# An 8192 x 8192 float32 transpose: two whole-row loads by GpSimd replaced by 26 small ones

## The chip, the core and the metric

The kernel runs on one core of one Trainium2 chip. The time is that of the device for one execution, in microseconds (us). The core has five engines that work side by side: TensorE (PE in the profile; its weight loads are PEld), VectorE (DVE), ScalarE (ACT), GpSimd (POOL) and SyncE (SP), which here only issues transfers. Transfers between the chip's memory and the core's on-chip memory run on 16 DMA engines. An instruction on SyncE puts a transfer into one queue (q1 in the profile, "SPq" where it is issued), one on GpSimd into another (q0, "POOLq"); both queues are served by the same 16 DMA engines. A transfer raises a semaphore by 16 in all when it has landed, one count for each DMA engine.

## The reference

```python
def setup_inputs():
    return {
        "x": np.random.randn(8192, 8192).astype(np.float32),
    }

def reference(x: np.ndarray) -> np.ndarray:
    return np.transpose(x)
```

256 MB (268.44 MB in the profile's unit) are read and as many written.

## The kernel before

**Tiling.** `x` is cut into T = 128 chunks of 128 rows by J = 4096 columns, 2048 KB each: chunk t holds the rows of c = t mod 64 and the left (t < 64) or right half of the columns. A chunk is loaded into a place of `arena`, 128 partitions of 16 KB. It has 16 ranges of 256 columns. TensorE transposes each range in two blocks of 128 x 128 against the identity `ident` (line 414), always every second column, into one of two PSUM tensors: ranges 0 to 7 into `pss[0]`, 8 to 15 into `pss[1]`. ScalarE empties the first and VectorE the second (`copies`, line 341), either into `slots`, where blocks wait, or straight into the place of the store that is next. VectorE then gathers what has been waiting into that place (`gather`, line 303). A store w (`store`, issued through `wide_dma`, line 28) writes one range of the last 16 chunks, 2048 KB again, so each of the 16 ranges is written every 16 chunks. At the start and the end, and where the left half turns into the right, stores are smaller or in two parts.

**Order.** SyncE issues everything in one order, made ahead: store t - 1, then load t + 2 (more loads ahead in the first ten chunks), and so on. It waits before each: before a store until its pieces have been copied, before a load until the place in `arena` is free (`free`, line 206). Such a wait holds up everything behind it on SyncE. `home` says where in `arena` a load or store lies, `before` whose place it takes over.

**Semaphores.** `s_ld` has one semaphore for each place of a chunk; a landed load adds 16, and TensorE waits for 16 and takes them away. `s_pe` counts TensorE's progress, 4 a chunk (5 in the last). `s_free` hands PSUM back to TensorE. In the chunks from E = 12 to LAST TensorE also runs two filler matmuls a chunk (line 408) on a PSUM tensor not in use, and from chunk 24 on ScalarE makes two filler copies a chunk (line 450) once the chunk has landed.

**The two loads apart.** Chunks 40 and 88 (`APART`) are loaded another way (`load_apart`). GpSimd loads PART = 120 of the 128 rows itself (line 231), SyncE the other 8 (line 234); GpSimd waits for both and then adds 16 to `s_ld` in the transfers' stead (line 240). Ahead of chunk 40, at the start of the kernel (line 394), GpSimd makes a load of 5 rows of 64 numbers into `spare`, and right ahead of chunk 88 one of 1 row (line 219, in `turn_engines`), and waits for its landing. Nothing reads `spare`. Apart from `ident`, made in the first microseconds, GpSimd has no other work.

## Time and profile before

| | us |
|---|---|
| median of 3 runs | 1283.3 |
| lowest and highest of them | 1281.83 and 1286.52 |
| the profiled execution | 1285.68 |
| its span, from the first to the last instruction | 1283.9 |
| mean granted clock of TensorE in it | 0.877 |

The page of the profile gives first each engine's busy time, its share of the span and its count of instructions. Then the span is cut into 40 equal slices of 32.1 us. In the rows of the engines and of DMA a digit is the busy share of a slice in tenths; GB/s is what the 16 DMA engines moved in it. The rows of the queues give packets, MB and the time that the packets took, as a share of the time of 16 engines. A group of instructions is shown as line, engine, operation, what it writes and reads, how often, then busy us, the mean ns of one, and how long the engine was idle before them. In a timeline a row is start, length, engine, line and operation; a "q" behind the engine means that its sequencer issued a transfer. In a view by stretches a row is the stretch, its length, each engine's busy time (and count of instructions), then the granted clock, the busy share of the 16 DMA engines and GB/s. It puts a packet wholly into the stretch in which it starts, so a share can be a little over 1.

### The profile page before, as it was taken

The page shows a single profiled execution, that of the slowest core. Times are in us where ns is not written, and L with a number is a line of the kernel's source. Part 1 is how long each engine was busy: PE and PEld are TensorE (multiplying, and loading weights), DVE is VectorE, ACT ScalarE, POOL GpSimd, SP SyncE. Part 2 cuts the span into 40 slices and gives each one's busy share as a digit, 9 for nine tenths or more (in the row PEclk, how much of TensorE's full clock was granted, in tenths as well). Part 3 has the DMA queues.
Part 4 walks back from the last instruction along what each step waited for, and adds up shares of the span by engine and source line. Part 5 has one row for each costly group of instructions (what it writes and reads, how often), then busy time and mean ns, then how long its engine had stood idle before and what let it go on. Part 6 is the DMA issues. An engine that isn't in the chain of part 4 may idle for free. (4 is left out here: it accounts for less than half of the span.)

```text
span 1283.9 us, 12050 instructions
## 1 busy us (share of the span) xinstructions
PE 850.2 (66%) x4552; PEld 648.6 (51%) x4552; DVE 614.8 (48%) x715; ACT 638.7 (50%) x606; POOL 4.0 (0%) x10
## 2 busy tenths in 40 slices
PE   6767777666656776677666776676666676666630
PEld 6655555544445555455445554455555554545430
DVE  3554544554444454454445544444544545445471
ACT  2321215566455556655655556555665555655510
POOL 0000000000000000000000000000000000000000
PEclk9988888989889888988899889879889978899865
DMA  9999999999999999999999999999999999999998
GB/s 395 414 427 431 429 431 430 431 428 431 359 403 417 431 431 431 430 432 430 428 429 429 424 422 430 382 402 430 432 432 429 430 423 403 426 429 419 407 384 336
DMA packets 41430, 537.10 MB, mean 418 GB/s; under 512 B 4672, under 2 KB 5312, under 8 KB 8384
## 3 DMA queue, kind: packets, MB, share of 16 engines
q1 hardware_dynamic: 41056, 532.96, 98.5%
q0 software_dynamic: 352, 3.93, 1.1%
q14 instruction: 18, 0.15, 0.0%
q8 instruction: 4, 0.07, 0.0%
HBM read 268.44 MB, written 268.44 MB: 418 GB/s over the span
## 5 line engine op out<-in xcount | busy, mean ns | idle before, releaser
L414 PEld LDWEIGHTS ps<-ident,arena 128*128 128x128 f32 x4096 | 559.0, 211 | 251.3 <-issue 250.6
L414 PE MATMUL ps<-ident,arena 128*128 128x128 f32 x4096 | 574.3, 304 | 138.9 <-PEq L411 138.9
L303 DVE COPY arena<-slots 128x2048 f32<-128x2048 f32 (+7 forms) x316 | 304.1, 1011 | 519.3 <-DMA out_dram<-arena 511.5
L408 PE MATMUL ps<-ident 128*128 128x512 f32 x456 | 282.4, 752 | 247.3 <-PEq L406 247.3
L450 ACT COPY ps<-ident 128x2048 f32<-128x2048 f32 x204 | 381.4, 1869 | 68.4 <-DMA arena<-in_x_dram 64.7
L341 ACT COPY slots<-ps 128x1024 f32<-128x1024 f32 (+2 forms) x335 | 238.3, 781 | 244.6 <-DVE arena L303 226.9
L341 DVE COPY slots<-ps 128x512 f32<-128x512 f32 (+2 forms) x336 | 289.2, 911 | 57.8 <-PE ps L414 56.4
L408 PEld LDWEIGHTS ps<-ident 128*128 128x128 f32 x456 | 89.5, 217 | 336.3 <-issue 336.3
L341 ACT COPY arena<-ps 128x256 f32<-128x256 f32 x66 | 24.5, 372 | 282.8 <-DVE arena L303 238.4
L341 DVE COPY arena<-ps 128x256 f32<-128x256 f32 x63 | 26.7, 424 | 69.5 <-PE ps L414 68.7
L231 POOL DMA_DIRECT2D arena<-in_x_dram x2 | 2.1, 1056 | 338.2 <-PE ps L414 332.6
L219 POOL DMA_DIRECT2D spare<-in_x_dram x2 | 1.1, 574 | 481.3 <-PE ps L414 481.1
L341 ACT ACT_TABLE_LOAD x1 | 1.3, 1283 | 1.0 <-SPq L160 1.0
L385 POOL TENSOR_SCALAR_AFFINE_SELECT ident<-ident 128x128 f32<-128x128 f32 x1 | 0.3, 287 | 0.2 <-POOL ident L383 0.2
L383 POOL MEMSET ident<- 128x128 f32 x1 | 0.2, 204 | 0.5 <-SPq L160 0.5
L492 POOL MEMSET const-bfloat16-1.0<- 128x1 bf16 x1 | 0.1, 101 | 0.0
L492 POOL MEMSET const-uint8-127<- 128x1 uint8 x1 | 0.1, 101 | 0.0
L492 POOL MEMSET const-float32-0.0<- 128x1 f32 x1 | 0.1, 98 | 0.2 <-issue 0.2
L492 POOL MEMSET const-float32-1.0<- 128x1 f32 x1 | 0.1, 98 | 0.0
## 6 DMA issues: line engine op xcount, KB each, us to landing
arena<-in_x_dram SPq DMA_DIRECT2D x126, 2048.0 KB, 20.3
out_dram<-arena SPq DMA_DIRECT2D x98, 2048.0 KB, 16.7
out_dram<-arena SPq DMA_DIRECT2D x4, 1920.0 KB, 12.3
out_dram<-arena SPq DMA_DIRECT2D x4, 1792.0 KB, 12.3
out_dram<-arena SPq DMA_DIRECT2D x4, 1664.0 KB, 13.2
out_dram<-arena SPq DMA_DIRECT2D x4, 1536.0 KB, 13.8
out_dram<-arena SPq DMA_DIRECT2D x4, 1408.0 KB, 13.1
out_dram<-arena SPq DMA_DIRECT2D x4, 1280.0 KB, 15.3
```

Of the source, the lines that this page charges most:

```text
L219: nc.gpsimd.dma_start(out=spare[:n, :], in_=x[:n, :64]).then_inc(s_gp, 16)
L231: nc.gpsimd.dma_start(out=arena[:PART, o:o + J], in_=x[c * P:c * P + PART, s * J:(s + 1) * J]).then_inc(s_gp, 16)
L303: cp = nc.vector.tensor_copy(out=ap(arena, do, [[P, len(v)], [dist, B], [1, P]]), in_=ap(slots, so, [[gap, len(v)], [P, B], [1, P]]),)
L341: cp = eng.copy(out=dst, in_=i) if e == 0 else eng.tensor_copy(out=dst, in_=i)
L383: nc.gpsimd.memset(ident, 0.0).then_inc(s_id, 1)
L385: nc.gpsimd.affine_select(out=ident, in_=ident, compare_op=mybir.AluOpType.not_equal, fill=1.0, base=0, pattern=[[-1, P]], channel_multipl ...
L408: nc.tensor.matmul(out=pss[1][:, :4 * P], lhsT=ident, rhs=four, start=True, stop=True)
L414: tr = nc.tensor.transpose(pss[h][:, (u * B + b) * P:(u * B + b + 1) * P], arena[:, q + b:q + PIECE - B + b + 1:B], ident,)
L450: cp = nc.scalar.copy(out=pss[0].rearrange("p (k i) -> p k i", i=P), in_=ap(ident, 0, [[0, J // 2 // P], [1, P]]))
L492: nc = _bacc.Bacc("TRN2", target_bir_lowering=False, num_devices=1)
```

## The change

Chunks 40 and 88 are loaded as all others are. `load_apart`, `turn_engines` and the semaphore `s_few` go. In place of the load of 5 rows at the start stands `small_loads`: GpSimd waits until TensorE is through with chunk 39 + k (k = 0 to 25; `s_pe` at 4 x (40 + k)), loads the first n rows and m columns of `x` into `spare`, and waits for the landing. `spare` becomes twice as wide. The 26 loads have between 1 and 120 rows, of 17 to 128 numbers.

```diff
-        spare = nc.alloc_sbuf_tensor("spare", [P, 64], dt).ap()
+        spare = nc.alloc_sbuf_tensor("spare", [P, 128], dt).ap()
...
-        s_few = nc.alloc_semaphore("s_few")
...
-        APART = (40, 88)
-        PART = P - P // 16
-        gp = [0]
-
-        def turn_engines(n):
-            nc.gpsimd.dma_start(out=spare[:n, :], in_=x[:n, :64]).then_inc(s_gp, 16)
-            gp[0] += 16
-            nc.gpsimd.wait_ge(s_gp, gp[0])
-
-        def load_apart(t):
-            s, c = divmod(t, CH)
-            o = home["L", t] * PIECE
-            for u in before["L", t]:
-                free(nc.sync, u)
-                free(nc.gpsimd, u)
-            if t > APART[0]:
-                turn_engines(1)
-            nc.gpsimd.dma_start(
-                out=arena[:PART, o:o + J], in_=x[c * P:c * P + PART, s * J:(s + 1) * J]
-            ).then_inc(s_gp, 16)
-            nc.sync.dma_start(
-                out=arena[PART:, o:o + J], in_=x[c * P + PART:(c + 1) * P, s * J:(s + 1) * J]
-            ).then_inc(s_few, 16)
-            gp[0] += 16
-            nc.gpsimd.wait_ge(s_gp, gp[0])
-            nc.gpsimd.wait_ge(s_few, 16 * (APART.index(t) + 1))
-            nc.gpsimd.sem_inc(s_ld[home["L", t]], 16)
+        FIRST = 40
+        shapes = [(n, 64) for n in (15, 30, 60, 90, 120, 105, 75, 45, 12, 24, 36, 48, 72, 7, 14, 28, 56, 112, 100)]
+        shapes += [(1, 17), (1, 34), (15, 64), (13, 64), (4, 64), (15, 128), (30, 128)]
+
+        def small_loads():
+            for k, (n, m) in enumerate(shapes):
+                nc.gpsimd.wait_ge(s_pe, 4 * (FIRST + k))
+                nc.gpsimd.dma_start(out=spare[:n, :m], in_=x[:n, :m]).then_inc(s_gp, 16)
+                nc.gpsimd.wait_ge(s_gp, 16 * (k + 1))
...
-            if t in APART:
-                load_apart(t)
-                return
...
-        turn_engines(5)
+        small_loads()
```

## The prediction

> **What bounds the kernel now.** I read the page first: the share of each engine, the slices, the DMA queues, the chain that ended last.

> ```profile
> span 1283.9 us, 12050 instructions
> PE 850.2 (66%) x4552; PEld 648.6 (51%) x4552; DVE 614.8 (48%) x715; ACT 638.7 (50%) x606; POOL 4.0 (0%) x10
> ...
> DMA  9999999999999999999999999999999999999998
> GB/s 395 414 427 431 429 431 430 431 428 431 359 403 417 431 431 431 430 432 430 428 429 429 424 422 430 382 402 430 432 432 429 430 423 403 426 429 419 407 384 336
> ...
> q1 hardware_dynamic: 41056, 532.96, 98.5%
> q0 software_dynamic: 352, 3.93, 1.1%
> ```

> No compute engine is busy for more than 66% of the span, while the packets of the SP queue (q1) alone fill 98.5% of the time of the 16 DMA engines. The kernel moves 537 MB, and in its undisturbed slices it moves them at 430 to 432 GB/s. So time is lost only where the GB/s row falls below 431, and it falls at the start, at slices 11 to 13 (from 321 us), at slices 26 and 27 (from 802 us) and at the end. The two holes in the middle are where chunks 40 and 88 are loaded. The busy row stays at 9 in them: the engines were not idle there, their packets took longer.

> Next I cut the span into stages at these holes. The columns behind the colon are the length, busy time and count of each engine, then the granted clock, the DMA share and GB/s.

> ```profile
> core 0: us, PE busy (x) PEld busy (x) DVE busy (x) ACT busy (x) POOL busy (x), PEclk, DMA share, GB/s
> 140.00:336.00 196.00, 134.32 (x720) 101.56 (x720) 96.71 (x112) 92.86 (x93) 0.54 (x1) 0.90 1.01 430
> 336.00:404.40 68.40, 42.69 (x216) 32.05 (x216) 27.95 (x32) 34.48 (x31) 0.00 (x0) 0.83 1.00 377
> 404.40:614.00 209.60, 150.09 (x760) 108.14 (x760) 102.11 (x117) 124.11 (x108) 0.00 (x0) 0.88 1.01 431
> 614.00:818.00 204.00, 140.08 (x752) 105.75 (x752) 100.93 (x123) 116.88 (x108) 0.51 (x1) 0.91 1.01 427
> 818.00:910.30 92.30, 64.52 (x324) 46.86 (x324) 41.35 (x48) 51.50 (x44) 1.57 (x1) 0.85 0.99 403
> 910.30:1043.90 133.60, 91.14 (x479) 68.29 (x480) 64.37 (x75) 78.41 (x70) 0.00 (x0) 0.91 1.01 431
> 1043.90:1110.40 66.50, 46.09 (x243) 34.59 (x241) 33.55 (x39) 36.45 (x35) 0.00 (x0) 0.87 0.99 411
> 1110.40:1183.80 73.40, 47.96 (x263) 36.65 (x264) 33.64 (x38) 43.88 (x38) 0.00 (x0) 0.95 1.01 428
> 1183.80:1210.60 26.80, 16.75 (x101) 13.71 (x99) 14.38 (x16) 13.38 (x12) 0.00 (x0) 0.94 1.00 397
> ```

> A stage of length t at g GB/s has lost t x (1 - g/431). The stage behind chunk 40 lost 68.4 x (1 - 377/431) = 8.6 us, the one behind chunk 88 lost 92.3 x (1 - 403/431) = 6.0 us. The stages between them lost 0 and 1.9 us. Two late stages lost 3.1 and 2.1 us with no GpSimd load near them; these matter below.

> The 16 engines are not equally far along. At the very end one of them works alone:

> ```profile
> 1278.00:1282.00 4.00, 0.00 (x0) 0.00 (x0) 0.00 (x0) 0.00 (x0) 0.00 (x0) 0.50 0.06 24
> ```

> A share of 0.06 is one engine of 16, for 4 us. A chunk counts as landed when its last engine is through, so this one sets the pace, and a mean over 16 engines can mislead. As a second account I therefore take the SyncE queue's own times of issue, since it issues in program order behind whatever landed last:

> ```profile
> 139.52 0.81 SPq L250 DMA_DIRECT2D arena<-in_x_dram  x1
> ...
> 335.03 1.20 SPq L234 DMA_DIRECT2D arena<-in_x_dram  x1
> ...
> 348.31 0.61 SPq L250 DMA_DIRECT2D arena<-in_x_dram  x1
> ...
> 368.84 0.33 SPq L250 DMA_DIRECT2D arena<-in_x_dram  x1
> ...
> 404.32 0.59 SPq L250 DMA_DIRECT2D arena<-in_x_dram  x1
> ...
> 481.31 0.59 SPq L250 DMA_DIRECT2D arena<-in_x_dram  x1
> ...
> 816.70 0.56 SPq L234 DMA_DIRECT2D arena<-in_x_dram  x1
> ...
> 998.35 0.59 SPq L250 DMA_DIRECT2D arena<-in_x_dram  x1
> ```

> From 139.52 to 335.03 lie 20 loads, 9.776 us each: one load and one store of 2 MB at 431 GB/s, 4.87 us each, with little over. Behind chunk 40 the next two loads come after 13.3 and 20.5 us. From 335.03 to 481.31 lie 14 loads in 146.3 us, where 14 x 9.776 = 136.9 would do: 9.4 us lost. From 404.32 to 816.70 the pace is 412.38 / 42 = 9.819 us, and from 816.70 to 998.35 lie 18 loads in 181.65 us against 18 x 9.819 = 176.7: 4.9 us lost. The two accounts agree, 14.6 us by bytes and 14.3 us by pace.

> **What the change removes.** Chunks 40 and 88 become loads like the other 126: 128 rows on the SP queue, signalled by their own landing and no longer through GpSimd. That takes away the mixing of the two queues on all 16 engines, the 8-row load of line 234, and the hole before chunk 88, where SyncE has issued its 8 rows while GpSimd still waits for its small load. I count the 14.3 us as gone: what made up the holes was data of those two loads beside data of q1, and nothing of that kind is left. What could not go is the data itself, but it is moved at 431 GB/s in either case and is in both accounts already. The bounds: if only the mixing itself vanished and half of the aftermath were due to other things, 7 us; if all of both holes and the late losses of 3.1 and 2.1 us are their doing, 14.6 + 5.2 = 19.8 us.

> The large GpSimd loads also did something useful: 120 rows are 15 engines' shares of 8 rows, so if the engine left out is the last one, it is spared 4.87 us. The pace account holds this gain already, because it is taken at the last engine: 14.3 us is the loss net of what was spared. But a spread that is never reset grows on. The late dips (3.1 + 2.1 = 5.2 us between 1043.9 and 1210.6, none between 910.3 and 1043.9) come when the last reset is long past. If the reset at chunk 88 is missing they start earlier; I put 100 us earlier, so 5.2 x 100/167 = 3.1 us more. This is a choice: no row shows what causes the dips. Bounds: 0, as between 404.4 and 614, where the rate is 431 for 210 us; and 397 GB/s, the worst stage, all the way from 818 to 1210.6, 392.6 x (1 - 397/431) = 31 us.

> **What it adds.** 26 loads by GpSimd, one behind each chunk from 40 to 65. Their rows sum to 1,128 and their data to 0.30 MB, which at 431 GB/s is 0.7 us. Data is not the price, packets are. The trace has two such loads, and one of them falls into the steady stream:

> ```profile
> q1 hardware_dynamic: 200, 2.95, 98.4%
> q0 software_dynamic: 32, 0.00, 0.3%
> ...
> spare<-in_x_dram POOLq DMA_DIRECT2D x1, 0.2 KB, 5.8
> ...
> L219 POOL DMA_DIRECT2D spare<-in_x_dram x2 | 1.1, 574 | 481.3 <-PE ps L414 481.1
> ```

> These are the queues between 816 and 823 us, the load's landing, and its group on the page. Its 32 packets (its landing counts 16, one notice for each engine, so 16 are data) took 0.3% of 16 engines' 7 us, 0.34 us in all or 10.5 ns each, while q1 kept 98.4%. The added loads have some 1,128 + 26 x 16 = 1,544 packets; at 10.5 ns over 16 engines that is 1.0 us, at most twice that if a row of 256 or 512 B takes longer than one of 16 B. I take 1.1 us. The far bound is the big GpSimd loads' price per row: 14.3 us over 240 rows, 0.060 us, times 1,128 rows is 67 us. That row is far in size (16 KB beside 256 B), the small load is near in everything but its number of rows, so I stand close to it.

> Nothing is queued behind them: GpSimd has no other work after its first microseconds. Its waits (for TensorE's count, then for the landing, 5.8 us inside a chunk's 9.8) delay only its own next load, and issuing takes 0.57 us each on an engine that is 0% busy. Were one late, it would meet the next chunk instead. The larger spare tile is only memory. The 5-row load that goes away at the start held up nobody but GpSimd itself.

> [...]

> **The sum**, against the profiled execution's own 1285.68 us (span 1283.9 and 1.8 around it): - 14.3 + 1.1 + 3.1 = - 10.1, so 1275.6 us. That execution is 2.4 us over the median of the three runs, 1283.3; on the median's footing it is 1273.2. I forecast 1273 us, with a range of its own from 1269 to 1280.

> **Rivals.**

> *The late dips take it back (no change).* Without a reset at chunk 88, the spread between the engines keeps growing, packets stretch as they do from 1043.9 us on, and the loss starts near 818 and runs on. At the mean rate of the two bad stages (66.5 us at 411 and 26.8 us at 397: 407), 200 us cost 200 x (1 - 407/431) = 11 us in place of 3.1, and the time is 1281. For it: the dips are there, they come late, and one engine is seen alone at the end. Against it: 210 us at full rate behind chunk 40, and 1110.4 to 1183.8 at 428, later than any reset.

> *The same mechanism at its worst (slower).* If everything from 818 to 1210.6 runs at 397 GB/s, 31 us are lost where 11.2 us were lost before (the 6.0 of the hole and 5.2). With the 9.4 us of chunk 40 gained and 1.1 us paid, the time is 1283.3 + 31 - 11.2 - 9.4 + 1.1 = 1295.

> *Small loads that cost like large ones (slower).* Where: the 16 DMA engines between 350 and 610 us, each time that q0 has work beside q1. At 0.060 us a row the time is 1283.3 - 14.3 + 3.1 + 67 = 1339. It decides from (14.3 - 3.1) / 26 = 0.43 us for each load on the last engine: from there on the change no longer pays, and over 0.68 us it is slower by more than 0.5%. For it: while q0 and q1 share the engines the rate drops by far more than q0's bytes explain. Against it: 32 packets of a small load in 7 us of steady stream, 0.34 us for all engines.

> *The whole loss was the big loads' doing (faster still).* If the late dips are an aftermath of chunk 88, their 5.2 us go as well and the 3.1 are not paid: 1283.3 - 19.5 + 1.1 = 1265. Against it: 133.6 us at 431 GB/s lie between.

> **How the numbers follow.** The forecast's mechanism has 0.54, the late dips with no net change 0.18, their worst case 0.08, dear small loads 0.10, the still faster case 0.10. A measurement of this kernel can tell about 0.5%, 6.4 us, from no change: faster is below 1276.9, slower above 1289.7. Of the forecast's 0.54 about 0.40 lie below 1276.9, and with the 0.10 of the fastest case faster has 0.50. The other 0.14 and the 0.18 make 0.32 for the same. The two slow cases make 0.18. The range of 8 in 10 leaves out these two and the last tip of the fast one: 1265 to 1287.

> **What would show it.** In the changed kernel the GB/s row should have no hole near 335 and 817 us; loads should be issued every 9.8 us through both places, and no load should come from GpSimd but the 26. Through 350 to 610 us, GB/s should stay at 429 or more; a fall to 405 there (6%) would be the dear small loads. In q0 the share should fall from 1.1% to about 0.1%. The last engine should run alone at the end for longer than 4 us, since it is spared less. If the stages from 818 us on lie under 415 GB/s, the growing spread was the larger thing and the forecast is wrong; if the holes stay without the big loads, my reading of them is wrong altogether.

## The result, and the profile after

| | before | changed |
|---|---|---|
| median of 4 runs, us | 1284.91 | 1272.1 |
| lowest and highest, us | 1281.83 and 1287.89 | 1269.73 and 1274.2 |
| ratio, with 95% interval | | 0.990 [0.9865, 0.9935] |
| the profiled execution, us | 1285.68 | 1269.73 |

The changed kernel is 1% faster; the forecast was 1273 us. Some executions of a kernel take several per cent longer than its others (of e2 one took 1327.55 us, another 1274.31), and medians and ratios from here on are of the others alone. These are lines of the changed kernel's page: span, slices and queues.

```profile
span 1267.9 us, 12095 instructions
...
GB/s 392 412 426 430 428 431 428 424 431 431 430 430 431 431 430 430 431 430 431 428 428 429 430 430 431 430 431 431 430 431 430 425 415 412 421 431 430 432 423 297
...
q1 hardware_dynamic: 41312, 536.89, 99.7%
q0 software_dynamic: 832, 0.30, 0.1%
```

The holes at slices 11 to 13 and 26 to 27 are gone. The next lines are the same stretches as before (length, busy time of each engine, granted clock, DMA share, GB/s).

```profile
336.00:404.40 68.40, 47.10 (x260) 34.96 (x259) 33.74 (x38) 40.33 (x37) 2.76 (x5) 0.93 1.01 432
404.40:614.00 209.60, 144.77 (x759) 105.00 (x760) 102.97 (x119) 122.98 (x110) 11.00 (x21) 0.90 1.01 430
614.00:818.00 204.00, 137.72 (x754) 102.72 (x752) 100.54 (x122) 118.79 (x110) 0.00 (x0) 0.92 1.01 430
818.00:910.30 92.30, 62.80 (x326) 46.76 (x327) 43.73 (x50) 54.70 (x46) 0.00 (x0) 0.90 1.01 431
910.30:1043.90 133.60, 91.08 (x491) 68.10 (x490) 64.72 (x73) 76.34 (x70) 0.00 (x0) 0.92 1.00 425
1043.90:1110.40 66.50, 47.33 (x249) 34.09 (x249) 32.38 (x39) 39.19 (x36) 0.00 (x0) 0.89 1.00 417
1110.40:1183.80 73.40, 48.68 (x271) 38.42 (x269) 37.15 (x44) 43.31 (x40) 0.00 (x0) 0.93 1.01 431
```

Behind chunk 40 the rate went from 377 to 432 GB/s, behind chunk 88 from 403 to 431. There are still late dips: 425 GB/s from 910.3 to 1043.9 us, where the kernel before ran at 431, and 417 from there to 1110.4. SyncE's queue gives the same picture by pace:

```profile
325.91 0.59 SPq L227 DMA_DIRECT2D arena<-in_x_dram  x1
...
394.56 0.60 SPq L227 DMA_DIRECT2D arena<-in_x_dram  x1
...
817.14 0.59 SPq L227 DMA_DIRECT2D arena<-in_x_dram  x1
...
906.99 0.59 SPq L227 DMA_DIRECT2D arena<-in_x_dram  x1
```

Seven loads lie between the first two rows, 9.81 us each, and nine between the last two, 9.98 us each, where single steps of 13.3, 20.5 and 16.5 us stood before.

The 26 small loads lie between 357 and 603 us. These are the queues from 340 to 610 us and the loads' group:

```profile
q1 hardware_dynamic: 7962, 115.89, 100.3%
q0 software_dynamic: 832, 0.30, 0.4%
...
L219 POOL DMA_DIRECT2D spare<-in_x_dram x26 | 13.8, 529 | 587.5 <-PE ps L391 587.5
```

0.4% of 270 us is 1.1 us for each DMA engine, all 26 loads together. The stretch that holds most of them, 404.4 to 614 us, runs at 430 GB/s.

### The profile page after: what moved, and what is told of

It reads as the page before. It is cut to its first block, busy times and chain, and to the rows that moved or that the text cites. A ratio compares the mean times of both kernels' runs of the same rounds, so it can differ in the third digit from the quotient of the medians.

```text
span 1267.9 us, 12095 instructions
## 1 busy us (share of the span) xinstructions
PE 834.6 (66%) x4552; PEld 635.5 (50%) x4552; DVE 614.8 (48%) x715; ACT 638.9 (50%) x606; POOL 14.5 (1%) x32
## 5 line engine op out<-in xcount | busy, mean ns | idle before, releaser
L391 PEld LDWEIGHTS ps<-ident,arena 128*128 128x128 f32 x4096 | 542.3, 211 | 248.4 <-issue 248.3
L391 PE MATMUL ps<-ident,arena 128*128 128x128 f32 x4096 | 556.3, 298 | 141.3 <-PEq L388 141.2
L385 PEld LDWEIGHTS ps<-ident 128*128 128x128 f32 x456 | 93.3, 226 | 333.6 <-issue 333.6
L219 POOL DMA_DIRECT2D spare<-in_x_dram x26 | 13.8, 529 | 587.5 <-PE ps L391 587.5
## 6 DMA issues: line engine op xcount, KB each, us to landing
out_dram<-arena SPq DMA_DIRECT2D x4, 1920.0 KB, 12.8
```

What stands on the lines that cost most here:

```text
L219: nc.gpsimd.dma_start(out=spare[:n, :m], in_=x[:n, :m]).then_inc(s_gp, 16)
L385: nc.tensor.matmul(out=pss[1][:, :4 * P], lhsT=ident, rhs=four, start=True, stop=True)
L391: tr = nc.tensor.transpose(pss[h][:, (u * B + b) * P:(u * B + b + 1) * P], arena[:, q + b:q + PIECE - B + b + 1:B], ident,)
```

## The experiments

Each ran on one chip beside the kernel before, and a ratio is to that kernel in the same set: the first four stand in one set, the next four in another, the last three in a third. Between sets the medians shift by a few us (the kernel before had 1282.1, 1286.6 and 1283.1), so ratios are compared, or medians within a set. "Loss" is by bytes against 431 GB/s in the two stretches, 336 to 404.4 us and 818 to 910.3 us, as in the prediction, and of one execution each.

| kernel | median, us | ratio [95% interval] | loss at 40 | loss at 88 |
|---|---|---|---|---|
| before | 1284.91 | | 8.6 | 6.0 |
| changed | 1272.1 | 0.990 [0.9865, 0.9935] | 0 | 0 |
| e1, no small loads | 1267.75 | 0.9885 [0.9837, 0.9933] | 0 | 0 |
| e2, apart at 40 only | 1279.37 | 0.9981 [0.9946, 1.0015] | 9.7 | 0 |
| e3, apart at 88 only | 1271.95 | 0.9916 [0.9883, 0.9949] | 0.2 | 6.4 |
| e4, 120 + 8 rows, SyncE's queue | 1273.36 | 0.9929 [0.99, 0.9959] | 2.2 | 5.4 |
| e5, 114 small loads | 1281.63 | 0.9973 [0.994, 1.0007] | 0.2 | 1.1 |
| e6, 128 rows by GpSimd | 1274.65 | 0.9898 [0.9842, 0.9954] | 1.7 | 4.1 |
| e7, 128 rows by SyncE, signal through GpSimd | 1269.62 | 0.986 [0.9814, 0.9905] | 0.2 | 1.1 |
| e8, 64 + 64 rows, SyncE's queue | 1274.2 | 0.9908 [0.9866, 0.9949] | 3.7 | 3.6 |
| e9, two halves of the columns, SyncE's queue | 1267.23 | 0.986 [0.981, 0.9911] | 0.2 | 0.9 |
| e10, changed again | 1270.24 | 0.9892 [0.9851, 0.9934] | 0 | 0.4 |
| e11, no small loads again | 1267.36 | 0.9872 [0.9833, 0.9911] | 0 | 0.2 |

**The parts of the change, one by one (e1 to e3).**

e1 takes the small loads out of the changed kernel:

```diff
-        small_loads()
```

> The changed kernel without its 26 small loads; GpSimd makes no transfer at all. Theory (big GpSimd loads were the whole loss, small ones cost 0.04 us each): 1.1 us under the changed kernel's 1272.1, about 1271 us, ratio to the kernel before 0.989. Rival (small loads are dear, 0.2 us and more each, and hide part of the gain): 1267 us or less. Rival (small loads help, by shifting the engines against each other): 1274 us or more.

Its ratio of 0.9885 stands beside the changed kernel's 0.990. The whole gain is there without the small loads, so they brought none of it. Its median of 1267.75 us lies nearer to the dear loads' 1267 than to the 1271 expected, but in another set than the changed kernel's; their price lies within the intervals and is taken up again below.

e2 and e3 keep one of the two loads apart, e3 with the 1-row load ahead of it and with 4 rows in place of 5 at the start:

```diff
-        APART = (40, 88)
+        APART = (40,)
```

> The kernel before with the load apart at chunk 40 alone, no small load ahead of chunk 88. Theory: the hole behind chunk 40 stays (8 to 9 us by bytes between 336 and 404 us) and the one behind 88 goes, so about 1271 + 9 = 1280 us. Rival (the holes are worth nothing by themselves, since the spared engine pays for them): 1285 us or more.

```diff
-        APART = (40, 88)
+        APART = (88,)
...
-            if t > APART[0]:
+            if t > 40:
...
-        turn_engines(5)
+        turn_engines(4)
```

> [...] Theory: full rate through 335 us, the hole stays behind 817 us, about 1271 + 5 = 1276 us. Rival (the reset at 88 is worth more than its hole once it comes alone): 1270 us or less.

The stretches behind chunk 40 and behind chunk 88, of e2:

```profile
336.00:404.40 68.40, 41.06 (x222) 30.68 (x221) 29.24 (x35) 34.83 (x32) 0.54 (x1) 0.88 0.98 370
...
818.00:910.30 92.30, 65.05 (x327) 46.24 (x328) 43.50 (x50) 54.95 (x46) 0.00 (x0) 0.88 1.01 431
```

and of e3, with the late stretch:

```profile
336.00:404.40 68.40, 47.12 (x247) 34.83 (x247) 33.98 (x38) 40.17 (x36) 0.00 (x0) 0.90 1.01 430
...
818.00:910.30 92.30, 59.65 (x302) 44.55 (x303) 40.40 (x47) 49.71 (x41) 0.00 (x0) 0.87 0.99 401
910.30:1043.90 133.60, 94.03 (x492) 71.87 (x491) 64.75 (x74) 76.61 (x70) 0.00 (x0) 0.89 1.01 424
1043.90:1110.40 66.50, 46.88 (x236) 34.49 (x237) 30.85 (x37) 38.34 (x34) 0.00 (x0) 0.87 0.99 406
```

Each load makes its own hole and not the other's. In medians of the set, chunk 40 alone costs 1279.37 - 1267.75 = 11.6 us, chunk 88 alone 4.2. The forecast had 9.4 and 4.9; e2's runs scatter from 1274.3 to 1284.9, so the first figure is loose. e2's rival (1285 or more) falls: at chunk 40 the spared engine doesn't pay for the hole. e3's rival (1270 or less) is only made unlikely, since e3's median is 1272 and the intervals of e1 and e3 overlap; its hole of 6.4 us by bytes speaks against it.

**What about the loads makes the holes (e4, e6 to e9).**

e4 keeps the split and the signal, and takes away GpSimd's queue:

```diff
-            if t > APART[0]:
-                turn_engines(1)
-            nc.gpsimd.dma_start(
+            nc.sync.dma_start(
                 out=arena[:PART, o:o + J], in_=x[c * P:c * P + PART, s * J:(s + 1) * J]
             ).then_inc(s_gp, 16)
...
-        turn_engines(5)
```

> The kernel before with the same split of chunks 40 and 88 into 120 and 8 rows and the same signal through GpSimd, but both pieces issued by SyncE into its own queue, and no GpSimd transfer at all. Theory (two queues mixed on the 16 engines make the hole): no slice under 425 GB/s at 335 and 817 us, about 1271 us or, if the engine that gets none of the 120 rows is the late one, up to 10 us less. Rival (the split, or SyncE's order held up by the signal through GpSimd, makes the hole): the holes stay, 1280 us or more.

Here my theory fell as the only cause: the expected 1271 us nearly came, but so did part of both holes. The two places where the 120 rows are moved, in q1 alone:

```profile
348.00:360.00 12.00, 8.63 (x40) 5.11 (x38) 4.72 (x4) 4.88 (x5) 0.00 (x0) 0.86 1.01 359
820.00:834.00 14.00, 8.43 (x36) 6.99 (x36) 4.58 (x6) 5.97 (x6) 0.00 (x0) 0.76 1.00 316
```

There is no second queue, the engines are busy throughout (share 1.01 and 1.00), and yet they move 359 and 316 GB/s. So there is something in the load itself. A new theory, B: it is the shape. 128 rows are 8 for each of 16 engines; 120 rows are 8 for each of 15 (in the kernel before, one of the 16 counts of chunk 40's 120 rows comes at 347.5 us, the other 15 from 354.3 to 357.2), so from some row on they would lie on other engines than in all other loads and stores, and engines would get in each other's way.

e6 is the opposite case, GpSimd's queue with the usual shape:

```diff
-            if t > APART[0]:
-                turn_engines(1)
             nc.gpsimd.dma_start(
-                out=arena[:PART, o:o + J], in_=x[c * P:c * P + PART, s * J:(s + 1) * J]
+                out=arena[:, o:o + J], in_=x[c * P:(c + 1) * P, s * J:(s + 1) * J]
             ).then_inc(s_gp, 16)
-            nc.sync.dma_start(
-                out=arena[PART:, o:o + J], in_=x[c * P + PART:(c + 1) * P, s * J:(s + 1) * J]
-            ).then_inc(s_few, 16)
             gp[0] += 16
             nc.gpsimd.wait_ge(s_gp, gp[0])
-            nc.gpsimd.wait_ge(s_few, 16 * (APART.index(t) + 1))
...
-        turn_engines(5)
```

> The kernel before with chunks 40 and 88 loaded whole, all 128 rows, by GpSimd; no split, no 8 rows from SyncE, no small loads; GpSimd still gives the signal. Theory A (two queues mixed on the 16 engines make the hole): holes as before at 335 and 817 us, 5 us and more each by bytes, about 1278 to 1284 us. Theory B, new since the split on SyncE's own queue showed holes too (it is the shape: 120 rows on 15 engines lay the rows to the engines in another way than 128 rows on 16, so that engines get in each other's way): no hole over 1 us, 1267 to 1270 us.

The stretches around the transfer and right behind it, of e6:

```profile
338.00:364.00 26.00, 15.83 (x72) 11.62 (x71) 9.49 (x10) 12.91 (x12) 0.00 (x0) 0.74 1.01 430
364.00:388.00 24.00, 18.24 (x110) 14.20 (x111) 14.52 (x18) 15.29 (x14) 0.00 (x0) 1.00 1.01 401
818.00:824.00 6.00, 2.38 (x20) 2.19 (x20) 4.85 (x6) 2.05 (x4) 0.00 (x0) 1.00 1.01 431
824.00:844.00 20.00, 13.20 (x66) 10.51 (x67) 7.07 (x6) 11.28 (x9) 0.00 (x0) 0.83 0.92 366
```

and that both queues were at work in it, between 336 and 390 us:

```profile
q1 hardware_dynamic: 1404, 20.43, 91.6%
q0 software_dynamic: 144, 2.10, 9.1%
```

While 2.1 MB of q0 run beside q1, the 16 engines move 430 GB/s, as ever. In the kernel before the first of these stretches reads:

```profile
338.00:364.00 26.00, 11.38 (x47) 7.00 (x46) 5.71 (x7) 7.93 (x8) 0.00 (x0) 0.70 1.01 329
```

Mixing by itself costs nothing while it lasts. Something is left behind it, 1.7 and 4.1 us, more than B expected (under 1 us); behind 824 us the engines are also short of work, with a share of 0.92. The median of 1274.65 us lies between the times of A and B, and 5.0 us over that of e7, the next kernel, which differs from e6 in the queue alone (their intervals overlap). So B is hardly the whole cause: a load through GpSimd's queue seems to have a price of its own, paid after the mixing. Between 336 and 390 us it landed 14.7 us after its issue, SyncE's five loads after 19.1 (median); what exactly it delays is open.

e7 is the control, with the detour of the signal alone:

```diff
-            if t > APART[0]:
-                turn_engines(1)
-            nc.gpsimd.dma_start(
-                out=arena[:PART, o:o + J], in_=x[c * P:c * P + PART, s * J:(s + 1) * J]
-            ).then_inc(s_gp, 16)
             nc.sync.dma_start(
-                out=arena[PART:, o:o + J], in_=x[c * P + PART:(c + 1) * P, s * J:(s + 1) * J]
-            ).then_inc(s_few, 16)
+                out=arena[:, o:o + J], in_=x[c * P:(c + 1) * P, s * J:(s + 1) * J]
+            ).then_inc(s_gp, 16)
...
-            nc.gpsimd.wait_ge(s_few, 16 * (APART.index(t) + 1))
...
-        turn_engines(5)
```

> The control: chunks 40 and 88 loaded whole by SyncE as all others, but with the signal to TensorE still passed on by GpSimd. Both A and B: no hole, 1267 to 1270 us, as without any GpSimd transfer. Rival (the detour of the signal holds up the chain and makes part of the hole): holes of 2 us and more at 335 and 817 us.

It lost 0.2 and 1.1 us and has the ratio 0.986, as far down as the kernels without any GpSimd transfer. The signal's way through GpSimd is not it.

e8 and e9 cut the load in two pieces in SyncE's queue, once by rows and once by columns. e8 is e4 with another cut:

```diff
-        PART = P - P // 16
+        PART = P // 2
```

> Chunks 40 and 88 loaded by SyncE in two pieces of 64 rows each on 16 engines, 4 rows an engine, signal through GpSimd. Theory A (only two queues make holes): no hole, 1267 to 1270 us. Theory B (each shape other than 128 rows on 16 engines lays the rows to the engines differently): holes of 2 to 6 us by bytes at 335 and 817 us, 1272 to 1279 us. If no hole shows, it is the 15 engines and not any other shape that matters.

e9 has these two pieces in place of the one load of e7:

```diff
+            for k, sem in enumerate((s_gp, s_few)):
+                nc.sync.dma_start(
+                    out=arena[:, o + k * J // 2:o + (k + 1) * J // 2],
+                    in_=x[c * P:(c + 1) * P, s * J + k * J // 2:s * J + (k + 1) * J // 2],
+                ).then_inc(sem, 16)
...
+            nc.gpsimd.wait_ge(s_few, gp[0])
```

> Chunks 40 and 88 loaded by SyncE in two pieces again, but cut by columns: each piece has all 128 rows and half of the columns, 8 rows an engine as in a whole load; signal through GpSimd. Theory B (what counts is how the rows lie on the engines): no hole at 335 and 817 us, rates of 429 GB/s and more where the two pieces of 64 rows had 230 to 260, 1267 to 1271 us. Rival C (two pieces in one queue make the hole, of whatever shape): rates under 300 GB/s for some 8 us at both places, 1273 us or more.

The pieces of 64 rows, in e8:

```profile
348.00:356.00 8.00, 4.53 (x34) 3.92 (x32) 4.69 (x4) 3.96 (x5) 0.00 (x0) 1.00 1.02 260
820.00:828.00 8.00, 2.37 (x9) 0.93 (x7) 1.73 (x3) 3.98 (x3) 0.00 (x0) 0.91 0.96 254
```

and the halves by columns, in e9, in the first of these stretches and a longer one at the second place:

```profile
348.00:356.00 8.00, 5.10 (x30) 3.85 (x31) 3.17 (x4) 4.23 (x4) 0.00 (x0) 1.00 1.00 427
818.00:828.00 10.00, 6.03 (x36) 4.59 (x36) 5.05 (x7) 6.06 (x8) 0.00 (x0) 1.00 1.02 433
```

Two pieces in one queue cost nothing when each has all 128 rows (427 and 433 GB/s). When each has 64, the same bytes on the same queue move at 60% of the rate, with the engines busy. So the cut by rows makes the slow stretch, and neither the number of pieces nor the queue does. That is the part of B that is shown. The rest of B, that rows lie on other engines and these meet, is an inference: no view has the engine of a row.

The packets in the traces tell whom the cut slows. A packet here is 16 KB, one row of a load, and takes 0.61 us undisturbed (0.31 for the 8 KB of e9's pieces); call it long if it takes over a tenth more. In e8, 116 packets between 347 and 359 us are long, 1.10 us on average, about as many as the two pieces have rows; in e9 none is. So in one queue the pieces slow hardly more than themselves. In two queues it is otherwise. In the kernel before, from 338 to 355 us, 111 of q0's 120 rows are long, and with them 109 of q1's 177 packets, of which at most 8 belong to the load apart. In e6, from 338 to 364 us, none of q0's 128 rows and one of q1's 554 packets is long.

1.10 us in place of 0.61 is 1.8 times. What makes these packets slow is not shown here.

**The price of the small loads (e5, e10, e11).**

```diff
-        FIRST = 40
+        FIRST = 12
...
-        shapes += [(1, 17), (1, 34), (15, 64), (13, 64), (4, 64), (15, 128), (30, 128)]
+        shapes = [(120, 64)] * 114
```

> The changed kernel with 114 small loads in place of 26, each of 120 rows of 64 numbers, one behind each chunk from 12 to 125: 13,680 rows, 12 times as many. Price of the prediction (10.5 to 18 ns a packet over 16 engines, 15,500 packets): 10 to 16 us above the changed kernel without small loads, about 1279 to 1285 us, ratio 0.998 to 1.002. Rival (price per row as of the big loads, 0.060 us): 800 us more. Rival (the engines hide packets this small): under 1271 us.

The whole queue of these loads in e5's page, and the same from 140 to 614 us:

```profile
q0 software_dynamic: 3648, 3.51, 0.8%
...
q0 software_dynamic: 1536, 1.48, 0.9%
```

e5 against e7, the kernel of its set in which GpSimd transfers nothing, is 12.0 us slower by medians and (0.9973 - 0.986) x 1286.6 = 14.5 us by ratios, within what was expected. By occupation, 0.8% of 1279.0 us is 10.2 us for each engine. The rival with the big loads' price per row, 800 us, is dead, and so is the one in which such loads are free. The packets are also not what I had counted: 3,648 are 32 for each load of 120 rows, 16 of data (15 of them of 2,048 bytes, eight rows each) and 16 of notice, the same 32 as of a load of one row.

e10 and e11 are the changed kernel with and without its 26 loads in one set:

> The changed kernel once more, on one chip with the same kernel without its small loads, to price the 26 small loads. By the prediction (1.1 us): 1 us over the kernel without them, which the interval can't tell from none. By the prices of the 114 larger ones (11 to 15 us for 13,680 rows): 0.9 to 1.2 us over it. Rival (the 4 us between the medians of the first two sessions are their doing): 4 us over it.

> The changed kernel without its 26 small loads, beside the run above: 1 us under it by the prediction, 4 us under it by the rival.

1270.24 against 1267.36 us, 2.9 us, with ratios whose intervals overlap widely. 12.0 to 14.5 us for 114 loads is 0.105 to 0.127 us a load, 2.7 to 3.3 us for 26; counted by rows it is 1.0 to 1.2 us for 1,128. The runs point to 1 to 3 us and can't choose.

## Why the prediction was right, point by point

**What bounds the kernel** held: no slice of the kernel before or of the changed one goes over 432 GB/s, and the time that was won is what the two stretches lost. By bytes they lost 14.6 us, and they now lose nothing. The pace account, taken at the last engine, gave 14.3. e11 and e1 measure the removal alone: 1283.06 - 1267.36 = 15.7 us in one set, 1282.09 - 1267.75 = 14.3 in another.

**"That takes away the mixing of the two queues"** named only part of the mechanism. e6 has the mixing without the cut by rows and runs at 430 GB/s through it; e4 and e8 have the cut without the mixing and fall to 359, 316 and 260. At chunk 40 both together are worse than either: from 338 to 364 us the kernel before lost 26 x (1 - 329/431) = 6.2 us, while all of e4's stretch behind chunk 40 lost 2.2. The packets say why: with two queues the cut load slows the other queue's rows too (109 of 177 packets are long). At chunk 88 the cut alone explains most (5.4 of 6.0 us). Why the two places differ is open. The forecast was right all the same, because the change removes both at once and the sum counted the whole hole. Had the change kept the 120 rows and moved them to SyncE's queue, the same reasoning would have promised 14 us, and e4 got 8.7 (1273.36 against 1282.09).

**What the spared engine is worth** was in the pace account already. That it doesn't pay for the hole is clear at chunk 40 (e2); at chunk 88 (e3) the cost of 4.2 us against e1 lies within the noise.

**"The late dips start earlier", 3.1 us.** In the changed kernel they do start earlier than before: from 1000 to 1043.9 us it runs at 417 GB/s, the kernel before at 430. But e3, which has the load at chunk 88, is at 410 there:

```profile
910.30:1000.00 89.70, 65.23 (x335) 49.02 (x335) 43.28 (x50) 51.82 (x49) 0.00 (x0) 0.87 1.01 431
1000.00:1043.90 43.90, 28.80 (x159) 22.84 (x157) 21.48 (x25) 24.79 (x21) 0.00 (x0) 0.92 1.00 410
```

So the missing reset can't be the whole reason. A slight sign for it is the stretch ahead, 910.3 to 1000 us: the three kernels in which GpSimd loads chunk 88 (before, e3, e6) run at 431 GB/s, the changed kernel at 430 and 429 (e10), and seven of the other eight at 424 to 429. The price did not show. All that is lost from 910.3 to 1210.6 us is 5.6 to 7.7 us in those three and 2.1 to 7.7 in the ten; the same changed kernel lost 4.2 in one execution and 7.7 in another (e10). An earlier start that costs 3.1 us more is not seen, and a term of - 1.4 us (4.2 - 5.6), as the two profiled executions have it, is no more certain. In these the time differs by 1285.68 - 1269.73 = 16.0 us where the sum had 10.1, and this term is 4.5 of the 5.9 between them. The spread between the engines does grow: from the first to the last of the 16 counts of a load's landing the changed kernel has 2.8 us from 150 to 200 us, 5.6 from 550 to 600 and 8.6 from 1000 to 1050 (medians), the kernel before 3.2, 6.5 and 8.4, with a fall from 8.6 shortly ahead of chunk 88 to 6.0 shortly behind it. But in the changed kernel it also falls with no reset, to 5.5 us from 1100 to 1150. What makes the dips stays open; no run aimed at it. It isn't a cut by rows alone: 161 packets of the changed kernel are long between 910 and 1110 us, where all loads have 128 rows.

**The small loads, 1.1 us**: the occupation of the engines is 1.1 us for each, as the sum had it, but by two errors that cancel. I counted 1,544 packets at 10.5 ns; there are 832, at 0.4% x 270 us x 16 / 832 = 21 ns. What they cost in time lies between 1.0 and 3.3 us by e5, so 1.1 may be too little by 2 us. GpSimd waits for each, 5.2 to 6.5 us to landing in the changed kernel, but nothing stands behind it.

**The rivals.** Dear small loads needed 0.43 us each to take the gain back; e5 has 0.11 to 0.13. The growing spread at its worst (1295 us) and with no net change (1281) did not come: 818 to 910.3 us run at 431. The fastest case (1265), the dips as an aftermath of chunk 88, falls with e11, whose median of 1267.4 is near it without the small loads, but whose trace still has dips between 910 and 1110 us:

```profile
910.30:1043.90 133.60, 90.80 (x500) 68.89 (x500) 65.36 (x75) 76.40 (x70) 0.00 (x0) 0.92 1.01 423
1043.90:1110.40 66.50, 48.00 (x233) 33.71 (x234) 32.44 (x39) 38.44 (x35) 0.00 (x0) 0.85 1.01 423
```

**The end.** I expected the last engine to run alone for longer than 4 us. From 1256 us on the changed kernel has

```profile
1256.00:1258.00 2.00, 0.00 (x0) 0.00 (x0) 0.00 (x0) 0.00 (x0) 0.00 (x0) 0.50 0.97 403
1258.00:1263.00 5.00, 0.00 (x0) 0.00 (x0) 0.00 (x0) 0.00 (x0) 0.00 (x0) 0.50 0.15 61
```

and the kernel before, ahead of the 4 us at 24 GB/s that the prediction shows,

```profile
1276.00:1278.00 2.00, 0.00 (x0) 0.00 (x0) 0.00 (x0) 0.00 (x0) 0.00 (x0) 0.50 0.75 310
```

A share of 0.15 is 2.4 engines of 16 on average, for 5 us, so it is not one engine that is left. The tail is a little longer and wider, and by bytes it lost as much as before: 4.4 us from 1256 to 1263 against 4.3 from 1276 to 1282. The end cost nothing of what was won.

**How near the number came** is in part luck. In medians of the same set the time fell by 1284.91 - 1272.1 = 12.8 us, where the sum had 10.1. The removal was worth up to 1.4 us more than counted and the dips' 3.1 us did not show, while the small loads may cost 2 us more.

**A better version.** Leaving out the small loads too gives 0.9885 and 0.9872 in two sets, clearly under the kernel before. Against the changed kernel it is 2.9 us better in one set, which its interval doesn't separate from equal.

## What to carry to other kernels

In a kernel bound by transfers, take the loss of a stretch as its length times the missing share of the full rate, take it a second time from the pace of the queue that issues, and count on it where the two agree: it priced the removal here within 2 us although only part of the mechanism behind it was known. To learn the mechanism, change the queue and the shape separately; one change that takes away both can't tell. And move whole tiles of 128 rows when the engines are full: a load cut by columns lost 0.2 and 0.9 us, one cut by rows into halves 3.7 and 3.6, and in a second queue a load cut by rows slowed the first queue's packets too (109 of 177).
